# A written-out order for TensorE: one 512-column matmul of the running product behind each narrow matmul, and shorter planned landing times

## The chip, the cores and the metric

One core of a Trainium2 chip. The metric is the time of one launch on the device in microseconds (us); the median of three runs of the kernel before is 1319.29 us (1318.65 to 1319.43). A measurement of this kernel can tell about 0.2% from no change, which is 2.6 us.

## What is computed

One layer of a streaming encoder on 512 tokens of width 2048, in float32. Cut to what matters:

```python
hn   = rmsnorm(x, norm_g)                             # (512, 2048)
proj = hn @ w_in                                      # three branches of q, k, v, gate (4 heads of 128),
                                                      # forget logits, three merge gates of width 2048
ya = forgetting_attention(rmsnorm(qa), rmsnorm(ka), va, f_logit)   # branch A, causal, 4 heads
yb = chunked_relpos_attention(rmsnorm(qb), rmsnorm(kb), vb, rel)   # branch B, causal by chunks, 4 heads
yc = stick_breaking_attention(qc, kc, vc)                          # branch C, strictly causal, 4 heads
ys = stack(ya, yb, yc) * silu(gate paths)
merged = sum_n sigmoid(gates_n) * (ys_n @ w_up_n)
out = x + merged @ w_out
```

Twelve heads in all (three branches of four), each with a 512 x 512 causal score matrix.

## The kernel before, in words

**Wide matmuls.** Every large product is done in pieces: an operand is split into a high and a low part, and each block costs three matmuls (high by high, low by high, high by low). All of them go through one helper, `mm` (L264, L265), and have 128 rows, a stationary operand of 128 x 128 and 512 moving columns. I call them *wide*; there are 5328 of that helper. Weights arrive as `raw` tiles (512 KB each, eight buffers), ScalarE makes the high part `wh` (L366) and VectorE the low part `wl` (L371). The input projection is computed in 24 column groups of 512; from the third on, two groups at a time go through a seven-product scheme (`Strassen`, L580) whose products 5, 7 need the difference of two weight tiles: the first tile is fetched by SyncE's queue (`fetch`, L276), and the second is added onto it in memory by a GpSimd DMA with accumulation (`add_up`, L280). Sums of two weight tiles are made on VectorE (L574).

**Narrow matmuls.** Beside this running product each head needs TensorE for small steps: transposes of 128 x 128 blocks (`turned` L801 for q, k and the gate path, `soft_trans` L926 for the attention weights, `turned_m` L1282 for the merged result), score products with 128, 256, 384 or 512 columns for query blocks 0 to 3 (`mm3`, L260 to L262, and a mask product L898 in branch A), and the products of weights with values with 512, 384, 256 and 128 columns (`av`, L1014 to L1016). I call those of under 512 columns *narrow*: 328 transposes, 72 products each of 128, 256 and 384 columns, and 16 mask products.

**What sets the order.** The order of the instructions on TensorE, ScalarE and VectorE is fixed when the program is built. `Flow` (L65 to L148) is a small planner: every piece of work is a task, a Python generator that yields either something to wait for (an `Event`, buffer `Slots`) or a step `(engine, cost)`. `Flow.run` takes the step that can start first by its own clocks, and among equal starts the one due first (the time when it became ready plus the task's slack). The running product is one task with a slack of 1e9 (`stream`, L1412), so it takes what the others leave; the heads' tasks have a slack of 5.0, in the last head 0.3 to 4.0. The planner's costs are `mm_us` (L151), `act_us`, `dve_us`, and its guess of when a transfer lands is `landing` (L270) and `add_up` (L280). In the kernel before a step on TensorE is a whole small group: four transposes are one step of 0.44, the three matmuls of a score block are one step. On the chip every engine works through its list in order, and waits by semaphores.

**The stages.** About 5 to 970 us: the projection, with one head's attention under way beside the next group's product. About 970 to 1033: the last head's attention (branch A, head 3) and, when its products are through, the first of the products with `w_up`. About 1033 to 1160: four column groups of `w_up` with sigmoid gates; these gates were stored to memory earlier (`gl`), are fetched again as `sg`, go through a sigmoid on ScalarE (L1232) after a load of the table for it, and are multiplied with the product's PSUM tile on VectorE (L1248), which frees the tile (`taken`, L1244). There are four such tiles (`acc`), so the four token blocks of one branch's product wait for the four multiplies of the branch before, in the order in which VectorE makes them. Each column group ends with 16 transposes into four PSUM tiles `att` (`turned_m`). About 1160 to 1318: the product with `w_out` in two seven-product tasks.

Of the kernel before, what the change touches and what calls it, by code (L numbers as in the profile page):

```python
# [15 lines left out]
P = 128  # L16
# [48 lines left out]
class Flow:  # L65
# [84 lines left out]

def mm_us(n, x=1):  # L151
    return x * max(0.115, n / 2400 + 0.0133)

# [10 lines left out]
def hybrid_kernel(  # L164
# [92 lines left out]

    def mm3(ps, lh, ll, rh, rl, start, stop, more=False):

        nc.tensor.matmul(ps, lh, rh, start=start, stop=False, skip_group_check=more)  # L260
        nc.tensor.matmul(ps, lh, rl, start=False, stop=False, skip_group_check=more)  # L261
        nc.tensor.matmul(ps, ll, rh, start=False, stop=stop, skip_group_check=more)  # L262

# [111 lines left out]
    def products(u, ps, kts, tbs, block, first=False, last=False, bank=None, done=None, outer=False):  # L375

        for group in [[tb] for tb in tbs] if outer else [tbs]:
# [4 lines left out]
            for j, kt in enumerate(kts):  # L382
                for tb in group:
                    yield lambda: block(kt, tb) is not None
                    h, lo, ev = block(kt, tb)
                    yield ev
                    yield PE, mm_us(S, 2)
                    mm(ps[tb], h, u.hi[:, j, :], first and j == 0)
                    mm(ps[tb], lo, u.hi[:, j, :])
            yield u.ready  # L390
# [354 lines left out]
    class Head:  # L745
# [50 lines left out]
        def turned(self, r):  # L796

            yield PE, 0.11 * QB
            ps = att()
            for tb in range(QB):  # L800
                nc.tensor.transpose(ps[:, blk(tb)], self.c[tb][:, blk(r)], identf)  # L801
            self.taken()
            return ps
# [81 lines left out]
        def soft_scores(self, i):  # L885
# [5 lines left out]
            (qh, ql), (kh, kl) = self.t[Q], self.t[K]  # L891
            yield PE, mm_us(m, 3) + (mm_us(P) if n == A else 0)
            ps = att()[:, :m]
            mm3(ps, qh[:, blk(i)], ql[:, blk(i)], kh[:, :m], kl[:, :m], True, n == B)
            p = self.p[i]
            mx, sm = small("mx"), small("sm")
            if n == A:
                nc.tensor.matmul(ps[:, blk(i)], identb, mska, start=False, stop=True)  # L898
            done = self.nth("s", QB)
# [16 lines left out]
        def soft_trans(self, j):  # L916
# [5 lines left out]
            yield atts, 1  # L922
            yield PE, 0.11 * (QB - j)
            ps = att()
            for i in range(j, QB):
                nc.tensor.transpose(ps[:, blk(i)], self.p[i][:, blk(j)], identf)  # L926
            if self.nth("t", QB):
# [15 lines left out]
        def stick_scores(self, i):  # L943
# [4 lines left out]
            (qh, ql), (kh, kl) = self.t[Q], self.t[K]  # L948
            yield PE, mm_us(m, 3)
            ps = att()[:, :m]  # L950
            mm3(ps, qh[:, blk(i)], ql[:, blk(i)], kh[:, :m], kl[:, :m], True, True)
            if self.nth("s", QB):
# [49 lines left out]
        def av(self, j):  # L1002
# [4 lines left out]
            else:  # L1007
                yield atts, 1
            yield PE, mm_us(S - j * P, 3)
# [4 lines left out]
            nc.tensor.matmul(o, vh[:, blk(j)], h, start=j == 0, stop=False)  # L1014
            nc.tensor.matmul(o, vl[:, blk(j)], h, start=False, stop=False)  # L1015
            nc.tensor.matmul(o, vh[:, blk(j)], lo, start=False, stop=j == QB - 1)  # L1016
            set_(self.event("o", j))
# [59 lines left out]
    def quad(parts, g, done, early=False):  # L1077
# [8 lines left out]
        def mms(kts):  # L1086
            def go(u):
# [9 lines left out]
                else:  # L1097
# [3 lines left out]
                    for part in range(3):  # L1101
                        if part == 2:
                            yield u.ready
                        for j, kt in enumerate(kts):
                            yield (raw_hi[kt], raw_ev[kt], raw_ev[kt])[part]
                            yield PE, mm_us(S, QB)
                            w = u.lo if part == 2 else u.hi
                            for tb in tbs:
                                mm(ps[tb], block(kt, tb)[part == 1], w[:, j, :], kt + part == 0)
                if early and (kts[-1] + 1) % 4 == 0:  # L1110
# [92 lines left out]
    def split_y(i):  # L1203
        def go():
# [70 lines left out]
    def turned_m(g, i):  # L1275
        for tb in range(QB):
            yield merged_ev[NB - 1, g, tb]
        yield atts, 1
        yield PE, 0.11 * QB
        ps = att()  # L1280
        for tb in range(QB):
            nc.tensor.transpose(ps[:, blk(tb)], merged[g, tb][:, blk(i)], identf)  # L1282
        turns[g] = turns.get(g, 0) + 1
# [208 lines left out]
```

## Time and profile before

| | |
|---|---|
| median of the runs | 1319.29 us |
| the profiled execution | 1319.42 us, span 1317.7 us |
| TensorE busy | 1307.4 us (99%), 6034 matmuls |
| VectorE, ScalarE, GpSimd busy | 78%, 57%, 7% |
| TensorE idle by the trace | 6.1 us in five waits |
| granted TensorE clock | 1.000 |
| DMA | 266 MB, mean 202 GB/s |

How to read it. A row of the timeline has a start and a length in us, the engine, the line, the operation, what it writes and reads, the shapes and, after x, how many equal ones were merged. TensorE has two rows of records: PE for the matmuls and PEld for the load of the stationary operand that goes ahead of each. A matmul's recorded length (some 390 ns for a wide one) is longer than what it costs in a stream, since matmuls overlap; what one costs is read from start to start. A row ends with the engine's idle time ahead of it, in brackets, and what ended it.

### The profile page before, as it was taken

How to read it: one execution, taken by the hardware profiler on the slowest of the kernel's cores; microseconds unless marked ns; L12 is line 12 of the kernel's file. 1: busy time of each engine (PE TensorE's matmuls, PEld its weight loads, DVE VectorE, ACT ScalarE, POOL GpSimd, SP SyncE). 2: the span in 40 equal slices, each digit the busy share in tenths (PEclk: the TensorE clock that was granted, in tenths of full speed). 3: DMA queues.
4: the chain of work that ended last, by engine and by line, in shares of the span. 5: the costliest groups of instructions: out<-in, count | busy, mean ns of one | idle time of the engine just before them, and what ended most of it. 6: DMA issues, size and time to landing. Idle time of an engine off the chain costs nothing.

```text
span 1317.7 us, 17190 instructions
## 1 busy us (share of the span) xinstructions
PE 1307.4 (99%) x6034; PEld 1078.6 (82%) x6034; DVE 1023.4 (78%) x1420; ACT 752.4 (57%) x1271; POOL 91.5 (7%) x115
## 2 busy tenths in 40 slices
PE   9999999999999999999999999999999999999998
PEld 7788888888888888888888888888887788878787
DVE  6877787887878777687776877778789668798667
ACT  7655464564557646566466664667558545454342
POOL 0000001110011101111011110111000000000110
PEclk9999999999999999999999999999999999999999
DMA  9745677866777757777577775777786656637883
GB/s 361 233 121 145 181 210 191 235 170 180 211 192 229 201 164 232 175 228 203 170 225 176 225 207 168 224 177 217 225 250 196 236 192 205 164 95 250 246 240 128
DMA packets 89063, 266.03 MB, mean 202 GB/s; under 512 B 11264, under 2 KB 11264, under 8 KB 88976
## 3 DMA queue, kind: packets, MB, share of 16 engines
q1 hardware_dynamic: 71552, 206.16, 46.1%
q0 software_dynamic: 14976, 54.53, 23.2%
q10 hardware_dynamic: 2448, 4.24, 0.8%
q8 instruction: 47, 0.77, 0.2%
q14 instruction: 40, 0.33, 0.1%
HBM read 245.19 MB, written 19.70 MB: 201 GB/s over the span
## 4 chain that ended last, share of the span: by engine, by line
PE 95%; DMA 2%; ACT 1%; DVE 1%; issue 0%; POOL 0%; ACTq 0%; POOLq 0%; DVEq 0%
PE acc L265 87%; DMA raw<-in_w_out 2%; PE att L801 1%; PE att L926 1%; PE att L260 1%; PE att L261 1%; PE att L262 1%; DMA raw<-in_w_col 1%; PE att L1016 1%; PE att L1015 1%; PE att L1282 1%; ACT wh L366 1%; PE att L265 1%; PE att L1014 0%; DMA sg<-gl 0%; DVE wl L371 0%
## 5 line engine op out<-in xcount | busy, mean ns | idle before, releaser
L371 DVE TENSOR_TENSOR wl<-raw,wh 128x1024 fp32r<-128x1024 f32 (+1 forms) x405 | 493.4, 1220 | 209.5 <-PE acc L265 122.7
L366 ACT ACTIVATE wh<-raw 128x1024 fp32r<-128x1024 f32 (+1 forms) x405 | 426.7, 1055 | 369.5 <-PE acc L265 283.2
L265 PE MATMUL acc<-wh,x 128*128 128x512 f32 x1664 | 429.5, 392 | 0.0
L265 PEld LDWEIGHTS acc<-wh,x 128*128 128x128 f32 x1664 | 308.8, 188 | 65.7 <-ACT xn L476 1.7
L265 PE MATMUL acc<-wh,t 128*128 128x512 f32 x1056 | 272.7, 391 | 0.0
L265 PE MATMUL acc<-wl,x 128*128 128x512 f32 x832 | 230.1, 390 | 0.0
L265 PEld LDWEIGHTS acc<-wh,t 128*128 128x128 f32 x1056 | 196.7, 188 | 40.3
L265 PEld LDWEIGHTS acc<-wl,x 128*128 128x128 f32 x832 | 155.8, 188 | 33.0 <-DVE wl L371 0.4
L265 PE MATMUL acc<-wl,t 128*128 128x512 f32 x528 | 149.3, 390 | 0.0
L281 POOL DMA_DIRECT2D raw<-in_w_col x88 | 76.3, 867 | 878.1 <-DMA raw<-in_w_col 198.2
L574 DVE TENSOR_TENSOR raw<-raw,raw 128x1024 f32<-128x1024 f32 x104 | 126.7, 1218 | 0.0
L265 PEld LDWEIGHTS acc<-wl,t 128*128 128x128 f32 x528 | 98.4, 188 | 19.6
L265 PE MATMUL acc<-wh,m 128*128 128x512 f32 x416 | 105.2, 390 | 1.5 <-ACT wh L366 1.4
L265 PE MATMUL acc<-wh,y 128*128 128x512 f32 x384 | 103.7, 390 | 1.3 <-DVE sg L1248 1.3
L265 PEld LDWEIGHTS acc<-wh,m 128*128 128x128 f32 x416 | 77.9, 188 | 18.5 <-ACT wh L366 2.3
L265 PEld LDWEIGHTS acc<-wh,y 128*128 128x128 f32 x384 | 71.7, 188 | 16.8 <-DVE sg L1248 2.2
L265 PE MATMUL acc<-wl,y 128*128 128x512 f32 x192 | 59.7, 391 | 0.0
L265 PE MATMUL acc<-wl,m 128*128 128x512 f32 x208 | 58.1, 390 | 0.1
L246 ACT ACTIVATE ah<-att 128x512 fp32r<-128x512 f32 (+3 forms) x48 | 21.0, 438 | 48.1 <-PE att L926 48.1
L265 PEld LDWEIGHTS acc<-wl,m 128*128 128x128 f32 x208 | 38.9, 188 | 8.5 <-DVE wl L371 0.5
L250 DVE TENSOR_TENSOR al<-att,ah 128x512 fp32r<-128x512 f32 (+3 forms) x48 | 23.5, 490 | 25.5 <-ACT ah L246 24.8
L265 PEld LDWEIGHTS acc<-wl,y 128*128 128x128 f32 x192 | 35.7, 188 | 7.3
(179 smaller groups left out, 1115.9 us busy)
## 6 DMA issues: line engine op xcount, KB each, us to landing
raw<-in_w_col SPq DMA_DIRECT2D x235, 512.0 KB, 5.0
raw<-in_w_col POOLq DMA_DIRECT2D x88, 512.0 KB, 8.0
raw<-in_w_out SPq DMA_DIRECT2D x40, 512.0 KB, 3.6
raw<-in_w_up SPq DMA_DIRECT2D x24, 512.0 KB, 3.6
sg<-gl SPq DMA_DIRECT2D x48, 256.0 KB, 5.0
raw<-in_w_out POOLq DMA_DIRECT2D x16, 512.0 KB, 5.9
gl<-u SPq DMA_DIRECT2D x22, 256.0 KB, 9.2
gl<-s SPq DMA_DIRECT2D x22, 256.0 KB, 4.6
```

The costliest lines, as they stand in the source:

```text
L246: nc.scalar.activation(hi, src, AF.Copy)
L250: nc.vector.tensor_sub(lo, src, f(hi))
L260: nc.tensor.matmul(ps, lh, rh, start=start, stop=False, skip_group_check=more)
L261: nc.tensor.matmul(ps, lh, rl, start=False, stop=False, skip_group_check=more)
L262: nc.tensor.matmul(ps, ll, rh, start=False, stop=stop, skip_group_check=more)
L265: nc.tensor.matmul(ps, w, x, start=start, stop=stop, skip_group_check=more)
L281: nc.gpsimd.dma_start(to, src, accum_op=ALU.add)
L366: nc.scalar.activation(u.hi, u.raw, AF.Copy)
L371: nc.vector.tensor_sub(u.lo, u.raw, f(u.hi))
L574: nc.vector.tensor_add(to.raw, to.raw, self.raw)
L801: nc.tensor.transpose(ps[:, blk(tb)], self.c[tb][:, blk(r)], identf)
L926: nc.tensor.transpose(ps[:, blk(i)], self.p[i][:, blk(j)], identf)
```

## The change

The diff, cut to its core (the left-out pieces do the same to the other callers):

```diff
 class Flow:
+        self.main = None
+        self.narrow = False
...
     def spawn(self, gen, slack, ready=None):
+        if slack > 1e8:
+            self.main = task
...
     def run(self):
+            main = self.main
+            full = (self.narrow and main is not None and main.engine == PE
+                    and main.ready <= self.clock[PE] + 0.02)
             for t in self.tasks:
+                if full and t.engine == PE and t is not main and t.slack >= 1:
+                    continue
...
+            if e == PE:
+                self.narrow = t is not self.main and t.cost < 0.2

-def mm_us(n, x=1):
-    return x * max(0.115, n / 2400 + 0.0133)
+def mm_us(n):
+    return n / 2400 + 0.0133
+TURN = 0.05

-    def mm3(ps, lh, ll, rh, rl, start, stop, more=False):
+    def mm3(ps, lh, ll, rh, rl, start, stop, m):
         nc.tensor.matmul(ps, lh, rh, start=start, stop=False)
+        yield PE, mm_us(m)
         nc.tensor.matmul(ps, lh, rl, start=False, stop=False)
+        yield PE, mm_us(m)
         nc.tensor.matmul(ps, ll, rh, start=False, stop=stop)

     def add_up(to, src, ready, kb):
-        line[1] = max(line[1], ready + 1.0) + kb / 170.0
-        return Event(line[1] + 2.5)
+        line[1] += kb / 250.0
+        return Event(max(line[1], ready) + 6.5)

         def turned(self, r):
-            yield PE, 0.11 * QB
+            yield PE, TURN
             ps = att()
             for tb in range(QB):
+                if tb:
+                    yield PE, TURN
                 nc.tensor.transpose(ps[:, blk(tb)], self.c[tb][:, blk(r)], identf)

     def split_y(i):                 # in its branch for all heads but the last
+                yield heads[i].event("y")
                 yield t2s, 1
```

So each matmul becomes a step of its own in the planner (the wide ones and those of `av`, `soft_scores`, `soft_trans`, `turned_m` too). After a step outside the running product that is planned at under 0.2, a further step outside it is passed over as long as the running product has a matmul ready, unless the task's slack is under 1. A transpose is planned at 0.05 instead of 0.11, a 128-column product at 0.067 instead of 0.115. The planned landing of an accumulating DMA is still 6.5 after the first tile has landed when the line is free, but the planner's line of transfers is held for 2.05 instead of 3.01 per 512 KB, and no longer moved on to that landing plus one. What is computed, the number of instructions and the buffers are the same.

Counted over TensorE's whole list, the narrow matmuls stood in 122 groups between wide ones before and stand in 532 now: 313 single transposes, 66 single products each of 128, 256 and 384 columns, 12 single mask products, and 12 longer groups, mostly in the last head.

The first place is on TensorE at the last column group of `w_up`: `sg` are the merged tiles being transposed, `att` the PSUM tiles that they go to, and `acc` tiles belong to the running product with `w_out`. Before:

```order
L265 MATMUL acc_10273<-wl_10239,m_1812_9425 128x512
L1282 MATMUL att_10289<-identf,sg_9863 128x128
L1282 MATMUL att_10289<-identf,sg_9865 128x128
L1282 MATMUL att_10289<-identf,sg_9909 128x128
L1282 MATMUL att_10289<-identf,sg_9911 128x128
L1282 MATMUL att_10294<-identf,sg_9863 128x128
```

and now:

```order
L281 MATMUL acc_10273<-wl_10239,m_1818_9450 128x512
L1310 MATMUL att_10289<-identf,sg_9876 128x128
L281 MATMUL acc_10274<-wl_10239,m_1818_9450 128x512
L1310 MATMUL att_10292<-identf,sg_9876 128x128
L281 MATMUL acc_10273<-wl_10239,m_1821_9470 128x512
L1310 MATMUL att_10295<-identf,sg_9876 128x128
L281 MATMUL acc_10274<-wl_10239,m_1821_9470 128x512
L1310 MATMUL att_10300<-identf,sg_9876 128x128
L281 MATMUL acc_10273<-wh_10238,m_1823_9485 128x512
L1310 MATMUL att_10289<-identf,sg_9882 128x128
```

The 16 transposes stood in one piece and filled one PSUM tile after the other; now a wide matmul stands behind each, and the four tiles are filled side by side, so that the first is full with the thirteenth transpose instead of the fourth.

The second place is on TensorE in the last head: `p` are the attention weights, `y` marks wide matmuls of the product with `w_up`, `ah`, `al`, `vh`, `vl` are the parts of weights and values. Around its last transpose (L926, now L948) there stood:

```order
L265 MATMUL acc_9076<-wh_9024,y_8531 128x512 x2
L926 MATMUL att_9165<-identf,p_8837 128x128
L1014 MATMUL att_9116<-ah_9121,vh_8860 128x256
L1015 MATMUL att_9116<-ah_9121,vl_8861 128x256
L1016 MATMUL att_9116<-al_9122,vh_8860 128x256
L265 MATMUL acc_9076<-wh_9024,y_8569 128x512 x2
```

and now:

```order
L281 MATMUL acc_9089<-wl_9048,y_8572 128x512
L948 MATMUL att_9183<-identf,p_8842 128x128
L1037 MATMUL att_9134<-ah_9145,vh_8858 128x256
L1039 MATMUL att_9134<-ah_9145,vl_8859 128x256
L1041 MATMUL att_9134<-al_9146,vh_8858 128x256
L1037 MATMUL att_9134<-ah_9126,vh_8858 128x128
L1039 MATMUL att_9134<-ah_9126,vl_8859 128x128
L1041 MATMUL att_9134<-al_9127,vh_8858 128x128
L281 MATMUL acc_9204<-wh_9046,y_8599 128x512 x2
```

Counted from the start of the program, 4112 wide matmuls stand ahead of this transpose before and 4128 now; the narrow matmuls of the last head ahead of it are the same ones.

The third place is on ScalarE behind that transpose: `ah` is its copy out of PSUM, then come the table load and the sigmoids. Before:

```order
L246 ACTIVATE ah_9097<-att_9165 128x128
L1232 ACT_TABLE_LOAD
L1232 ACTIVATE sg_9123<-sg_9123 128x512
L1232 ACTIVATE sg_9125<-sg_9125 128x512
L1232 ACTIVATE sg_9127<-sg_9127 128x512
L1232 ACTIVATE sg_9129<-sg_9129 128x512
L246 ACTIVATE y_9136<-y_8961 128x2x256
L1232 ACTIVATE sg_9131<-sg_9131 128x512
L1232 ACTIVATE sg_9133<-sg_9133 128x512
L366 ACTIVATE wh_9206<-raw_8915 128x1024
L1232 ACTIVATE sg_9137<-sg_9137 128x512
L1232 ACTIVATE sg_9139<-sg_9139 128x512
```

and now:

```order
L260 ACTIVATE ah_9126<-att_9183 128x128
L1258 ACT_TABLE_LOAD
L1258 ACTIVATE sg_9147<-sg_9147 128x512
L1258 ACTIVATE sg_9149<-sg_9149 128x512
L1258 ACTIVATE sg_9151<-sg_9151 128x512
L1258 ACTIVATE sg_9153<-sg_9153 128x512
L260 ACTIVATE y_9103<-y_8947 128x2x256
L1258 ACTIVATE sg_9155<-sg_9155 128x512
L1258 ACTIVATE sg_9157<-sg_9157 128x512
L1258 ACTIVATE sg_9159<-sg_9159 128x512
L1258 ACTIVATE sg_9161<-sg_9161 128x512
L1258 ACTIVATE sg_9164<-sg_9164 128x512
```

The chain is the same but for one `wh`, which stood after the sixth sigmoid and now stands ahead of the `ah` of the first row. In both lists the ninth sigmoid (sg_9142, the row that follows those shown of before, and sg_9164, the last one shown now) is the one for VectorE's third multiply.

On SyncE's queue 19 of 501 rows have moved, most by one to four places; GpSimd's list is unchanged.

More of the change, by code (lines that the diff above doesn't have):

```diff
@@ L256, in minus @@
         nc.vector.scalar_tensor_tensor(to, a, -1.0, b, op0=ALU.mult, op1=ALU.subtract)
-    def mm3(ps, lh, ll, rh, rl, start, stop, more=False):
-        nc.tensor.matmul(ps, lh, rh, start=start, stop=False, skip_group_check=more)
-        nc.tensor.matmul(ps, lh, rl, start=False, stop=False, skip_group_check=more)
-        nc.tensor.matmul(ps, ll, rh, start=False, stop=stop, skip_group_check=more)
+    def mm3(ps, lh, ll, rh, rl, start, stop, m):
+        nc.tensor.matmul(ps, lh, rh, start=start, stop=False)
+        yield PE, mm_us(m)
+        nc.tensor.matmul(ps, lh, rl, start=False, stop=False)
+        yield PE, mm_us(m)
+        nc.tensor.matmul(ps, ll, rh, start=False, stop=stop)
     def mm(ps, w, x, start=False, stop=False, more=False):
@@ L386, in products @@
                     yield ev
-                    yield PE, mm_us(S, 2)
+                    yield PE, mm_us(S)
                     mm(ps[tb], h, u.hi[:, j, :], first and j == 0)
+                    yield PE, mm_us(S)
                     mm(ps[tb], lo, u.hi[:, j, :])
@@ L891, in soft_scores @@
             (qh, ql), (kh, kl) = self.t[Q], self.t[K]
-            yield PE, mm_us(m, 3) + (mm_us(P) if n == A else 0)
+            yield PE, mm_us(m)
             ps = att()[:, :m]
-            mm3(ps, qh[:, blk(i)], ql[:, blk(i)], kh[:, :m], kl[:, :m], True, n == B)
+            yield from mm3(ps, qh[:, blk(i)], ql[:, blk(i)], kh[:, :m], kl[:, :m], True, n == B, m)
             p = self.p[i]
@@ L922, in soft_trans @@
             yield atts, 1
-            yield PE, 0.11 * (QB - j)
+            yield PE, TURN
             ps = att()
             for i in range(j, QB):
+                if i > j:
+                    yield PE, TURN
                 nc.tensor.transpose(ps[:, blk(i)], self.p[i][:, blk(j)], identf)
@@ L948, in stick_scores @@
             (qh, ql), (kh, kl) = self.t[Q], self.t[K]
-            yield PE, mm_us(m, 3)
+            yield PE, mm_us(m)
             ps = att()[:, :m]
-            mm3(ps, qh[:, blk(i)], ql[:, blk(i)], kh[:, :m], kl[:, :m], True, True)
+            yield from mm3(ps, qh[:, blk(i)], ql[:, blk(i)], kh[:, :m], kl[:, :m], True, True, m)
             if self.nth("s", QB):
@@ L1008, in av @@
                 yield atts, 1
-            yield PE, mm_us(S - j * P, 3)
+            n = mm_us(S - j * P)
+            yield PE, n
             if j == 0:
@@ L1278, in turned_m @@
         yield atts, 1
-        yield PE, 0.11 * QB
+        yield PE, TURN
         ps = att()
         for tb in range(QB):
+            if tb:
+                yield PE, TURN
             nc.tensor.transpose(ps[:, blk(tb)], merged[g, tb][:, blk(i)], identf)
```

5 lines of the change are left out of this document (4 added, 1 removed).

## The prediction, made blind

> **What bounds the kernel now.** I read the page first, then the waits of TensorE, then the timeline around narrow matmuls, and last the places where TensorE waits.
>
> ```profile
> span 1317.7 us, 17190 instructions
> PE 1307.4 (99%) x6034; PEld 1078.6 (82%) x6034; DVE 1023.4 (78%) x1420; ACT 752.4 (57%) x1271; POOL 91.5 (7%) x115
> ...
> PE att L417 <- DVE identb L310: 1.9, 1, 1.9
> PE acc L265 <- ACT wh L366: 1.4, 1, 1.4
> PE acc L265 <- DVE sg L1248: 1.3, 1, 1.3
> PE att L265 <- DVE wl L371: 1.1, 1, 1.1
> PE att L801 <- ACT w L793: 0.4, 1, 0.4
> ```
>
> TensorE is the bound all the way: it waits five times, 6.1 us together, and 1.9 of them are the start. So the change can pay in two ways only: a narrow matmul gets cheaper on TensorE, or one of the four later waits goes. It can cost in the same two ways. The price of a wide and of a narrow matmul is read from start to start (the first row is from the chain that ended last, the others from the timeline):
>
> ```profile
> 118.90 43.59 PE acc L265 x192
> ...
> 115.25 0.27 PE L926 MATMUL att<-identf,p 128*128 128x128 f32 x1
> 115.28 0.36 PE L1014 MATMUL att<-ah,vh 128*128 128x256 f32 x1
> 115.48 0.28 PE L1015 MATMUL att<-ah,vl 128*128 128x256 f32 x1
> 115.60 0.28 PE L1016 MATMUL att<-al,vh 128*128 128x256 f32 x1
> ...
> 115.03 0.14 PEld L926 LDWEIGHTS att<-identf,p 128*128 128x128 f32 x1
> 115.26 0.19 PEld L1014 LDWEIGHTS att<-ah,vh 128*128 128x128 f32 x1
> 115.36 0.19 PEld L1015 LDWEIGHTS att<-ah,vl 128*128 128x128 f32 x1
> ...
> 1053.54 1.08 PE L265 MATMUL acc<-wh,y 128*128 128x512 f32 x4
> 1054.46 1.91 PE L1282 MATMUL att<-identf,sg 128*128 128x128 f32 x16
> 1056.12 0.70 PE L265 MATMUL acc<-wl,y 128*128 128x512 f32 x2
> 1056.66 0.63 PE L265 MATMUL acc<-wh,y 128*128 128x512 f32 x2
> ...
> 63.03 0.40 PE L265 MATMUL acc<-wh,x 128*128 128x512 f32 x1
> 63.26 0.60 PE L801 MATMUL att<-identf,c 128*128 128x128 f32 x4
> 63.62 0.71 PE L265 MATMUL acc<-wh,x 128*128 128x512 f32 x2
> 64.17 0.86 PE L265 MATMUL acc<-wl,x 128*128 128x512 f32 x3
> ```
>
> A wide one costs 43.59 / 192 = 0.227. From 1053.54 to 1056.66 lie six wide ones (1.36) and 16 transposes, so those cost 1.76, or 0.110 each. That is twice what their 128 columns would cost by the wide rate (a 256-column product takes 115.60 - 115.48 = 0.12, a wide one 0.107 more for 256 more columns, so 128 columns should take about 0.066).
>
> The middle rows are the case that the change makes everywhere: a single transpose with a wide matmul ahead of it and a broader one behind. Its weights were loaded from 115.03 on, in the shadow of the wide one ahead of it. But the load for the matmul behind it starts at 115.26, a hundredth after the transpose itself, though the load unit had been free for a while, and the next load starts 0.10 later. From the transpose to the second 256-column product it takes 115.48 - 115.25 = 0.23, and 0.12 of that is the first such product. So the single transpose still costs 0.11: the load behind it has only the transpose to hide under, and it is longer than that. A narrow matmul pays for the load that comes after it, not for its own, whatever stands there.
>
> **TensorE's own work.** The change leaves the numbers of matmuls as they are: 328 transposes and 72 products of 128 columns at 0.11. What it changes is the number of groups, 122 to 532. A change between narrow and wide costs a little: the 16 transposes took 1.76, which is 0.01 over 16 x 0.109; the four at 63.26 took 64.17 - 63.03 - 3 x 0.227 = 0.46, which is 0.02 over 4 x 0.109. Of the 410 new groups 287 have a 128-column matmul in them, at 0.01 each 2.9. The other 123 are single products of 256 and 384 columns, long enough to cover a load; I take half the price, 0.6. Sum +3.5. Bounds: nothing, if the price belongs to a long stretch and not to each group; 410 x 0.023 = 9.4 by the group of four. I take the price of the sixteen, since its two ends are measured over the longer stretch, and by the single transpose above (0.11 in all) the price cannot be much higher.
>
> **The wait for the sigmoids.** It ends with the second row here:
>
> ```profile
> 1024.06 0.27 PE L926 MATMUL att<-identf,p 128*128 128x128 f32 x1
> ...
> 1033.01 1.19 PE L265 MATMUL acc<-wh,y 128*128 128x512 f32 x4 [1.28 <-DVE sg L1248]
> ...
> 1024.37 0.28 ACT L246 ACTIVATE ah<-att 128x128 fp32r<-128x128 f32 x1 [1.65 <-PE att L926]
> 1024.66 1.28 ACT L1232 ACT_TABLE_LOAD   x1
> ...
> 1029.62 1.05 ACT L366 ACTIVATE wh<-raw 128x1024 fp32r<-128x1024 f32 x1
> 1030.57 3.22 ACT L1232 ACTIVATE sg<-sg 128x512 f32<-128x512 f32 x6
> ...
> 1032.26 1.29 DVE L1248 TENSOR_TENSOR sg<-acc,sg 128x512 f32<-128x512 f32 x2 [1.12 <-ACT sg L1232]
> ```
>
> The chain is: the last head's last transpose (1024.06), its copy on ScalarE, the table load, nine sigmoids with a `y` and a `wh` among them, the third multiply on VectorE (1032.26), the PSUM tile, TensorE at 1033.01. In the new order that transpose has 16 more wide matmuls ahead of it (4128 for 4112), 16 x 0.227 = 3.6 later, because the four blocks' score products now take turns and end together, and the softmax and the transposes behind them start later. On ScalarE the chain behind it is shorter by the `wh` (1030.57 - 1029.62 = 0.95). The wait ends 3.6 - 0.95 = 2.7 later, and the wide matmuls that TensorE has until then are the same ones, merely done earlier, so nothing covers it: +2.7. Queued behind the late sigmoids on ScalarE are the `wh` of the units two ahead, with some 5 us to spare. Bounds: -1.5, if the whole wait went (no reason for it in the order), and +3.6 without the `wh`.
>
> **Two other waits.** The first row below starts four transposes that wait for ScalarE's scaling; they and the wide one behind them cost 998.54 - 997.05 (996.14 + 4 x 0.227), which is 1.05 over 4 x 0.11. Now wide matmuls stand between them and the first waits one wide matmul longer, but the others not at all: -0.3.
>
> ```profile
> 996.14 1.08 PE L265 MATMUL acc<-wh,x 128*128 128x512 f32 x4
> 997.58 0.62 PE L801 MATMUL att<-identf,w 128*128 128x128 f32 x2 [0.36 <-ACT w L793]
> ...
> 998.54 0.71 PE L265 MATMUL acc<-wl,x 128*128 128x512 f32 x2
> ...
> 1171.83 1.07 PE L265 MATMUL att<-wh,m 128*128 128x512 f32 x4
> 1174.03 1.19 PE L265 MATMUL att<-wl,m 128*128 128x512 f32 x4 [1.13 <-DVE wl L371]
> ...
> 1172.16 0.69 DVE L250 TENSOR_TENSOR m<-m,m 128x512 fp32r<-128x512 f32 x1
> 1172.76 1.22 DVE L371 TENSOR_TENSOR wl<-raw,wh 128x1024 fp32r<-128x1024 f32 x1
> ```
>
> The wait at 1174.03 costs 1174.03 - 1171.83 - 4 x 0.227 = 1.3. It is VectorE's queue: five splits of merged tiles (`m`, 0.6 each from 1172.16 to 1172.76) stand ahead of that `wl`. Now the four PSUM tiles fill side by side, so these tiles come later, and the new list has none of the five ahead of that `wl`. 5 x 0.6 = 3.0 less in the queue covers 1.3, but the first copy out of PSUM comes some 12 x 0.34 - 3 x 0.11 = 3.7 later and leaves VectorE fewer things to do meanwhile. I take the wait as gone, -1.3, with +1 as the other bound.
>
> **The planned landing times** move little but the planner's opinion: SyncE's list keeps its order but for 19 rows, GpSimd's is the same, and the loads wait for free `raw` tiles on the chip. The wait for the second `w_out` task is a chain of two transfers of about 10 us each (rows of the chain); its start is a `wl` that follows TensorE's own progress, so it stays: 0, give or take 1.5.
>
> ```profile
> 1223.12 9.65 DMA raw<-in_w_out
> ...
> 1233.33 10.52 DMA raw<-in_w_out
> ...
> raw<-in_w_col POOLq DMA_DIRECT2D x88, 512.0 KB, 8.0
> ```
>
> **The sum.** 3.5 + 2.7 - 0.3 - 1.3 = +4.6 on the profiled execution's 1319.42 (a span of 1317.7 and 1.7 around it), 1324.0; the median of the runs, 1319.29, is 0.13 below, so 1323.9. About 0.2%, or 2.6 us, is what a measurement here can tell.
>
> **The rivals.**
>
> *The narrow matmuls get cheap.* If TensorE can hold the load for the matmul after next while a wide one runs, a narrow matmul between wide ones costs only its columns, 0.066 instead of 0.11. Then 400 x 0.044 = 17.6 goes, and with +1.1 from the waits the time is 1302.8. Against it: the load rows at 115.26 and 115.36, and in all the trace no load that runs two ahead. For it: a single transpose with a wide (not a 256-column) matmul behind it is not in the trace. The Trainium skill, "TensorE: Matmul & The Clock Gate", section "Back-to-back issue gap", speaks for this rival: it gives about 56 ns for a matmul of 128 columns by itself and about 81 ns in a stream of loads and matmuls, pipelined through a reorder window. By these figures the time would come out as an estimated 1299 to 1309; the trace's 0.11 for a single transpose agrees with neither. My chance for this rival is 0.08.
>
> *No change that can be told.* The price of a change belongs to stretches (0 instead of 3.5): 1319.3 + 1.1 = 1320.4. Or both terms are half of what I reckon: 1319.3 + 1.75 + 1.35 - 1.6 = 1320.8. For it: the price was read from hundredths of a microsecond; against it: both groups show it with the same sign. 0.22.
>
> *Much slower.* The planner now thinks TensorE faster (0.05 for 0.11) and an accumulating DMA to land 6.5 after the first tile, where the last row above says 8.0 from issue to landing; ScalarE and VectorE work in order, so a `wh` put too early holds all behind it. TensorE is two units (5 us) behind these, so single delays of 1.5 are covered; were one of 1 us in each of the eleven later heads not, it is 1323.9 + 11 = 1335; were the price of a change the 0.023 of the group of four, 1319.3 + 9.4 + 1.1 = 1329.8. Against it: ScalarE waits for these transfers now too, without TensorE waiting for ScalarE there. 0.10.
>
> That the change does not do what it says is excluded by the order: 313 single transposes stand between wide matmuls.
>
> **How the numbers follow.** Forecast 0.60, cheap 0.08, no change 0.22, much slower 0.10. Faster by over 0.2% are the first rival and 0.03 of the forecast, should several waits go that I leave standing: 0.11; within 0.2% are the 0.22; slower is the rest, 0.67. The range 1317.5 to 1330.5 leaves out the cheap case, the last of the good luck and half of the much slower one.
>
> **What would show it.** In the new profile: the start of a wide matmul behind a single transpose comes about 0.12 later than without the transpose, so a pair of both takes about 0.35 (0.29 if the first rival is right); the load behind it starts with the transpose; TensorE's wait for `sg` has grown from 1.3 to about 4, in one or two places; the wait for `wl` at the start of `w_out` is gone; the wait for `raw` near the second task is still there. If pairs take 0.29, the whole prediction is wrong; if they take 0.35 and the time is below 1321, the sigmoid chain is where to look.

## The result, and the profile after

The changed kernel takes 1324.46 us (median of 5 runs, 1324.09 to 1327.19), the kernel before beside it 1319.29. The ratio is 1.0042, with a 95% interval of 1.0029 to 1.0056. The forecast was 1323.9. The profiled execution took 1324.79 (span 1323.1).

The head of the page, and then the waits of TensorE (in all, how often, the longest):

```profile
span 1323.1 us, 17158 instructions
PE 1310.8 (99%) x6034; PEld 1073.6 (81%) x6034; DVE 1023.0 (77%) x1420; ACT 754.2 (57%) x1271; POOL 91.5 (7%) x115
...
PE acc L281 <- DVE sg L1274: 3.3, 2, 1.7
PE att L434 <- DVE identb L326: 1.9, 1, 1.9
PE acc L281 <- ACT wh L382: 1.1, 1, 1.1
PE acc L281 <- DVE wl L387: 0.8, 1, 0.8
PE att L1037 <- ACT ah L260: 0.4, 1, 0.4
PE att L281 <- DVE wl L387: 0.3, 1, 0.3
PE att L1041 <- DVE al L264: 0.2, 1, 0.2
PE att L281 <- ACT wh L382: 0.2, 1, 0.2
```

The two pages differ by 32 instructions (17190 before): all of them are semaphore instructions, and every engine's own work has the same number of instructions. TensorE is busy 3.4 us longer for the same 6034 matmuls, and waits 8.2 us instead of 6.1. The wait for the sigmoids grew from 1.3 to 3.3. The 1.1 for `wl` at the start of `w_out` and the 0.4 for `w` went. Five small rows stand for waits at new places.

What a wait costs, and what the matmuls cost among themselves, can be read together from one series: the start of the k-th wide matmul of the helper `mm`, of which all kernels have the same 5328. The table gives that start for the kernel before, and for other kernels how much later it comes (us; the other kernels are those of the experiments below):

| k | before | after | rule off | landing alone | old prices | longer turns | turns whole | gates first | rule in heads |
|---|---|---|---|---|---|---|---|---|---|
| 0 | 6.14 | +0.21 | +0.20 | -0.43 | +0.20 | +0.21 | +0.21 | -0.01 | +0.21 |
| 20 | 10.80 | +0.70 | +0.68 | -0.42 | +0.62 | +0.59 | +0.79 | -0.04 | +0.67 |
| 4000 | 991.12 | +3.16 | +0.97 | -0.06 | +3.11 | +3.05 | +3.25 | +0.28 | +3.13 |
| 4040 | 1002.74 | +1.60 | -0.62 | -1.65 | +1.52 | +2.42 | +1.86 | -1.31 | +1.55 |
| 4152 | 1035.86 | +4.96 | +1.60 | -0.98 | +4.63 | +4.46 | +5.37 | -2.52 | +2.67 |
| 4660 | 1156.37 | +5.32 | +1.58 | -0.98 | +5.00 | +4.83 | +5.34 | -2.52 | +2.64 |
| 4700 | 1167.21 | +5.47 | +1.61 | -0.98 | +5.15 | +4.98 | +5.37 | -2.52 | +2.67 |
| 4730 | 1175.53 | +3.95 | +1.28 | -0.99 | +3.63 | +3.46 | +4.71 | -2.54 | +2.02 |
| 4850 | 1202.73 | +6.08 | +1.30 | -0.98 | +7.28 | +5.22 | +4.71 | -2.54 | +2.02 |
| 5327 | 1313.33 | +5.40 | +1.40 | -1.88 | +6.04 | +4.21 | +4.09 | -3.14 | +0.97 |

Read down the column "after": 0.70 is lost by k = 20, ahead of any narrow matmul of a head. The loss then grows while the heads' narrow matmuls alternate with wide ones (to k = 4000), changes in steps in the last head (4000 to 4152), grows a little with the 64 transposes of the merged product (to 4700), falls where the `wl` wait was, and rises again soon after.

Two cautions on the table. First, a row compares like with like only where as many narrow matmuls lie ahead of it. That is so in every row but k = 4040: there the kernel before has done four transposes more than all the others, which is 0.44 of each fall from 4000 to 4040. Second, the loss by k = 20 is one of the clock. The trace's record of the granted clock begins, at full, 5.91 us after the start in the kernel before and 7.44 in the changed one, and the first wide matmuls of the latter start 0.57, 0.43 and 0.28 apart, then 0.23. In all six traces of kernels built on the changed one that record begins at 7.15 to 7.64, in the four others at 4.80 to 6.23. No run here shows what sets it.

The alternation itself, at the last transposes of the merged product. First TensorE's matmuls, then its loads of stationary operands:

```profile
1162.84 0.27 PE L1310 MATMUL att<-identf,sg 128*128 128x128 f32 x1
1162.87 0.48 PE L281 MATMUL acc<-wl,m 128*128 128x512 f32 x1
1163.19 0.27 PE L1310 MATMUL att<-identf,sg 128*128 128x128 f32 x1
```

```profile
1162.84 0.19 PEld L281 LDWEIGHTS acc<-wl,m 128*128 128x128 f32 x1
1162.97 0.14 PEld L1310 LDWEIGHTS att<-identf,sg 128*128 128x128 f32 x1
1163.19 0.19 PEld L281 LDWEIGHTS acc<-wl,m 128*128 128x128 f32 x1
```

A pair takes 1163.19 - 1162.84 = 0.35 (0.344 over longer stretches), not 0.29, and the load of the wide one's operand starts with the transpose. A lone transpose costs 0.344 - 0.227 = 0.117.

The sigmoid wait, on TensorE, ScalarE and VectorE:

```profile
1029.62 0.27 PE L948 MATMUL att<-identf,p 128*128 128x128 f32 x1
...
1033.29 1.19 PE L281 MATMUL acc<-wh,y 128*128 128x512 f32 x4 [1.66 <-DVE sg L1274]
...
1037.97 1.20 PE L281 MATMUL acc<-wh,y 128*128 128x512 f32 x4 [1.65 <-DVE sg L1274]
```

```profile
1029.35 1.06 ACT L382 ACTIVATE wh<-raw 128x1024 fp32r<-128x1024 f32 x1 [0.43 <-PE acc L281]
1030.31 0.26 ACT L260 ACTIVATE ah<-att 128x128 fp32r<-128x128 f32 x1
1030.59 1.28 ACT L1258 ACT_TABLE_LOAD   x1
1031.88 2.19 ACT L1258 ACTIVATE sg<-sg 128x512 f32<-128x512 f32 x4
```

```profile
1037.23 1.29 DVE L1274 TENSOR_TENSOR sg<-acc,sg 128x512 f32<-128x512 f32 x2 [1.91 <-ACT sg L1258]
```

The last transpose comes 5.56 later than before; without the 3.16 that TensorE was late already, 2.4. The `wh` that no longer stands among the sigmoids stands ahead of the `ah` now and keeps it until 1030.31, 0.69 after the transpose, where it was 0.31 before. The third multiply comes 4.97 later.

### The profile page after: what moved, and what is told of

Read it like the earlier page. It is cut to its first block, busy times and chain, and to the rows that moved or that the text cites. A ratio compares the mean times of both kernels' runs of the same rounds, so it can differ in the third digit from the quotient of the medians.

```text
span 1323.1 us, 17158 instructions
## 1 busy us (share of the span) xinstructions
PE 1310.8 (99%) x6034; PEld 1073.6 (81%) x6034; DVE 1023.0 (77%) x1420; ACT 754.2 (57%) x1271; POOL 91.5 (7%) x115
## 4 chain that ended last, share of the span: by engine, by line
PE 98%; DVE 1%; ACT 1%; issue 0%; POOL 0%; DVEq 0%; ACTq 0%; POOLq 0%
PE acc L281 91%; PE att L820 1%; PE att L948 1%; PE att L281 1%; DVE wl L387 1%; PE att L276 1%; PE att L278 1%; PE att L1310 1%; PE att L274 1%; PE att L1037 1%; PE att L1041 1%; PE att L1039 1%; ACT sg L1258 0%; PE att L434 0%; PE att L1141 0%; ACT wh L382 0%
## 5 line engine op out<-in xcount | busy, mean ns | idle before, releaser
L281 PE MATMUL acc<-wh,x 128*128 128x512 f32 x1664 | 456.8, 402 | 0.0
L281 PE MATMUL acc<-wh,t 128*128 128x512 f32 x1056 | 283.5, 393 | 0.0
L281 PE MATMUL acc<-wl,x 128*128 128x512 f32 x832 | 233.6, 393 | 0.0
L281 PE MATMUL acc<-wh,y 128*128 128x512 f32 x384 | 106.9, 397 | 3.3 <-DVE sg L1274 3.3
```

The lines of the kernel that those rows point to most:

```text
L281: nc.tensor.matmul(ps, w, x, start=start, stop=stop, skip_group_check=more)
```

## The experiments

There were two theories at the start: **load** (the alternation itself costs TensorE time, and it delays the last head's transposes, so the rule is the cause) against **planner** (the new prices or landing times put ScalarE's and VectorE's work in a worse order).

**1. The rule off** (the changed kernel, its steps and prices kept; the narrow matmuls stand in 157 groups):

```diff
-            full = (self.narrow and main is not None and main.engine == PE
+            full = (False and main is not None and main.engine == PE
```

> The changed kernel without the rule that puts a wide matmul behind each narrow one; its single steps, planned costs and planned landing times stay. By the order the narrow matmuls then stand in 157 groups instead of 532 (135 instead of 400 with a 128-column matmul in them), and the last head's last transpose has 4121 wide matmuls ahead of it instead of 4128. Load theory (a narrow matmul pays for the weight load behind it, and each group costs about 0.01 us at its ends): 265 x 0.01 + 110 x 0.005 = 3.2 us less on TensorE, and the sigmoid wait ends up to 7 x 0.227 = 1.6 us earlier: 1324.5 - 3.2 - 1.6 = 1319.7, between 1318.5 and 1321.3. Planner theory (the alternation itself costs nothing; the new planned costs and landing times put ScalarE's and VectorE's work in a worse order): nothing that it names is undone, so 1323.5 or more.

Measured: 1319.83 (1318.66 to 1320.80), ratio 1.0000 (0.9991 to 1.0009). All of the loss is gone, with the prices and landing times still in. Load stands. In the table this column still ends at +1.40: its trace, the slowest of these runs, has 0.68 of that by k = 20, and from 1031.42 us its granted clock stands at half for 3.41 us (the mean from 1030 to 1040 is 0.83, in the kernel before and the changed one 1.00).

**2. The landing times alone** (the kernel before with the new `add_up`):

```diff
-        line[1] = max(line[1], ready + 1.0) + kb / 170.0
-        return Event(line[1] + 2.5)
+        line[1] += kb / 250.0
+        return Event(max(line[1], ready) + 6.5)
```

> The kernel before with the changed kernel's planned landing of accumulating DMAs alone. By the order there are 136 groups instead of 122, and the last head's last transpose has 4114 wide matmuls ahead instead of 4112. Load theory: 14 x 0.01 + 2 x 0.227 = 0.6 us more, 1319.9, between 1319 and 1321. Planner theory with the landing times as the cause: the larger part of the 5.2 us, 1322 or more.

Measured: 1318.03 (1317.51 to 1319.18), ratio 0.9988 (0.9979 to 0.9997). A small gain, where 1319.9 (1319 to 1321) was expected. The table shows its places. Between k = 4000 and 4040 it falls by 1.6; 0.44 of this is the four transposes still to come, the rest is the wait of the last head's transposes for ScalarE's scaling, and over the whole last head (to 4152) 0.9 remains. Another 0.9 goes at the second `w_out` task. There two traces of one kernel, that of experiment 6, differ by 0.4, so the size of this second part is not certain.

**3. The old prices** (the changed kernel with 0.11 for a transpose and 0.115 as the least for a product; still 532 groups):

```diff
-    return n / 2400 + 0.0133
+    return max(0.115, n / 2400 + 0.0133)
-TURN = 0.05
+TURN = 0.11
```

> The changed kernel with the old planned prices of narrow matmuls (0.115 at least, 0.11 for a transpose), the rule and the landing times as changed. The order of narrow and wide matmuls is the same in number: 532 groups, 4128 wide ones ahead of the last head's last transpose; ScalarE's and VectorE's lists differ. Load theory: TensorE's own work and the sigmoid wait stay, 1324.5 give or take 1.2 for the waits in the last product. Planner theory with the prices as the cause: with prices that fit the chip the order is good again, 1321.5 or less.

Measured: 1325.01 (1323.35 to 1325.45), ratio 1.0037 (1.0024 to 1.0050). That is within the 1324.5 give or take 1.2 of the load theory. The prices are not the cause; planner falls.

**4. Longer turns in the last head** (there a task of the last head with a slack under 1 keeps its due time for a further step on TensorE, so that the blocks' products no longer take turns; the last transpose has 4118 wide ones ahead of it):

```diff
                 task.engine, task.cost = w[:2]
+                if task.slack < 1 and task.engine == task.prev == PE:
+                    return
```

> The changed kernel, but in the last head (slack under 1) a step on TensorE that follows another one of the same task keeps that one's due time, so the four blocks' score products no longer take turns. By the order 529 groups, and the last transpose has 4118 wide matmuls ahead instead of 4128. Load theory with the sigmoid chain: the same price on TensorE, and the wait for the sigmoids ends up to 10 x 0.227 = 2.3 us earlier: 1322.2, between 1321.7 and 1323.3, with TensorE's wait for the gate tiles at 1 to 2 us instead of 3.3. If that wait is not set by this transpose: 1324.5.

Measured: 1323.07 (1321.43 to 1324.56), ratio 1.0026 (1.0017 to 1.0034); the wait for `sg` is 2.5 us. The time lies in the range expected, but near its end, and the wait is longer than the 1 to 2 expected. The rows on ScalarE say why:

```profile
1028.96 1.28 ACT L1260 ACT_TABLE_LOAD   x1
1030.25 0.63 ACT L1260 ACTIVATE sg<-sg 128x512 f32<-128x512 f32 x1
1030.95 0.63 ACT L262 ACTIVATE y<-y 128x512 fp32r<-128x512 f32 x1
1031.49 1.05 ACT L384 ACTIVATE wh<-raw 128x1024 fp32r<-128x1024 f32 x1
1032.44 5.81 ACT L1260 ACTIVATE sg<-sg 128x512 f32<-128x512 f32 x11
```

The table load starts 1.63 earlier than in the changed kernel, but a `y` and a `wh` (1.5 together) now stand ahead of nearly all sigmoids. And the wait for ScalarE's scaling came partly back (+2.42 at k = 4040 in the table, for +1.60).

**5. The turns of the merged product whole.** The rise between k = 4730 and 4850 was in no term of the forecast. The changed kernel shows there, on TensorE, VectorE, ScalarE and on SyncE's loading queue:

```profile
1206.41 0.73 PE L281 MATMUL acc<-wl,m 128*128 128x512 f32 x2 [0.81 <-DVE wl L387]
```

```profile
1186.14 1.22 DVE L591 TENSOR_TENSOR raw<-raw,raw 128x1024 f32<-128x1024 f32 x1
...
1188.21 1.22 DVE L591 TENSOR_TENSOR raw<-raw,raw 128x1024 f32<-128x1024 f32 x1
...
1203.39 0.69 DVE L672 TENSOR_TENSOR u<-u,xr 128x512 f32<-128x512 f32 x1 [1.51 <-DMA xr<-in_xn]
1204.01 2.35 DVE L387 TENSOR_TENSOR wl<-raw,wh 128x1024 fp32r<-128x1024 f32 x2
```

```profile
1203.24 1.06 ACT L382 ACTIVATE wh<-raw 128x1024 fp32r<-128x1024 f32 x1 [2.77 <-DMA raw<-in_w_out]
```

```profile
1166.56 27.02 SPq L293 DMA_DIRECT2D raw<-in_w_out  x5
```

So `wl` waits for `wh` and for `xr`, both wait for transfers, and the queue that issues them stood most of 27 us for five blocks. Its own waits between 1160 and 1215 say for what, in the changed kernel and in the kernel before:

```profile
SPq L293 <- DVE raw L591: 35.1, 4, 15.6
...
SPq L277 <- DVE raw L574: 41.4, 5, 15.9
```

These are VectorE's sums of `raw` tiles, the two at 1186.14 and 1188.21 above. The queue stands as long for them in the kernel before; what differs is when they come. There the same two are:

```profile
1179.47 1.22 DVE L574 TENSOR_TENSOR raw<-raw,raw 128x1024 f32<-128x1024 f32 x1
...
1181.91 1.22 DVE L574 TENSOR_TENSOR raw<-raw,raw 128x1024 f32<-128x1024 f32 x1
```

They come 6.7 and 6.3 later, TensorE only 3.95. The order of the queue differs too. In the kernel before the first `xr` stands ahead of the fifth block, in the changed kernel behind it (first before, then now), and so it is issued 9.7 later:

```profile
1163.68 19.86 SPq L277 DMA_DIRECT2D raw<-in_w_out  x4
1183.94 0.33 SPq L277 DMA_DIRECT2D xr<-in_xn  x1
...
1193.67 0.98 SPq L293 DMA_DIRECT2D xr<-in_xn  x2
```

The edit puts the four transposes of a tile in one piece again, too long for the rule:

```diff
-        yield PE, TURN
+        yield PE, TURN * QB
         ps = att()
         for tb in range(QB):
-            if tb:
-                yield PE, TURN
             nc.tensor.transpose(ps[:, blk(tb)], merged[g, tb][:, blk(i)], identf)
```

> The changed kernel, but the transposes of the merged product (64 in all) stand four in a piece again, planned at 0.2 us for a piece, so that the rule leaves them alone. What it is to tell: where the two waits of 2.1 us in all come from that the changed kernel's TensorE has 31 to 45 us after the last of these transposes, and that no term of the forecast held. Theory (spread transposes): one to a 512-column matmul, the last 16 take 15 more such matmuls (3.4 us) to be done; the splits of the product follow late, the sums of raw blocks stand behind them on VectorE, the loading queue waits for those, and blocks of w_out land late. Then with the pieces whole the two waits go (-2.1), the wait for wl of the kernel before comes back in front of them (+1.4), and 48 groups fewer give 0.4 back: 1324.5 - 1.1 = 1323.4 (1322.9 to 1323.9). Rival (the shorter planned landing times place these loads too late): the waits stay and only the 0.4 is seen, 1324.1.

Measured: 1322.60 (1321.36 to 1323.74), ratio 1.0022 (1.0013 to 1.0031). Three rows of TensorE's waits in it:

```profile
PE att L434 <- DVE identb L326: 1.9, 1, 1.9
PE acc L281 <- ACT wh L382: 1.2, 1, 1.2
PE att L281 <- DVE wl L387: 0.6, 1, 0.6
```

and the same two sums:

```profile
1184.90 1.22 DVE L591 TENSOR_TENSOR raw<-raw,raw 128x1024 f32<-128x1024 f32 x1
...
1187.51 1.22 DVE L591 TENSOR_TENSOR raw<-raw,raw 128x1024 f32<-128x1024 f32 x1
```

The sums are 5.4 and 5.6 later than before, TensorE 4.71. The rise is gone: between k = 4730 and 4850 the table has +4.71 and +4.71. The `wl` wait came back at half its size. The median is below the range expected (1322.9 to 1323.9): it differs by 1.9 from the changed kernel's, not by 1.1; by the table the end is 1.3 earlier. Spreading the transposes is the cause of the rise. By which way is open: the edit brings the sums forward, and it also puts the loading queue back in the order of the kernel before. The rise stands in the three traces with the moved order (changed kernel, experiments 3 and 4) and in none of the others. That late sums and late loads lead to it is read from the traces; the two were not tried apart.

This trace, too, has a stretch of half clock: 3.41 us from 1035.05, just behind the first sigmoid wait. Four wide matmuls take 1036.80 - 1035.09 = 1.71 there, 0.43 each:

```profile
1035.09 1.91 PE L281 MATMUL acc<-wh,y 128*128 128x512 f32 x4
1036.80 1.05 PE L281 MATMUL acc<-wl,y 128*128 128x512 f32 x2
```

It hides most of the second sigmoid wait, which is 0.41 in this trace instead of 1.65.

**6. Block C's gates first** (kernel before, new landing times, and in `gates_of` the first column group's other gates take a tile only when C's four have one):

```diff
+        if g == 0 and n != C:
+            for e in first_gates:
+                yield e
         yield t2s, 1
         t = sig[n, g, tb] = t2("sg")
+        if g == 0 and n == C:
+            set_(first_gates[tb])
```

> The kernel before with the new landing times, and one thing of its own: of the first column group's twelve gates, the four that are multiplied first (block C) take their tiles, and so their places in ScalarE's list, ahead of the other eight; before, two of the four stood ninth and tenth. Theory (TensorE waits there for the sigmoids' order, not for their start): the sigmoid wait of 1.7 us goes and nothing takes its place, 1318.0 - 1.7 = 1316.3 (1315.8 to 1317.0), 0.9975 of the kernel before. Rival (ScalarE has too much there in any order, so the next block's gates are late instead): 1317.5 to 1318.2, with a wait for sg a few us further on.

Measured: 1316.60 (1315.74 to 1317.15), ratio 0.9977 (0.9967 to 0.9986). The row for the sigmoids among TensorE's waits:

```profile
PE acc L265 <- DVE sg L1254: 0.2, 1, 0.2
```

It was their order, not how many there are. This version is faster than both kernels, by 3.0 than the kernel before.

**7. What is left: the rule in the heads**, that is the changed kernel with the edits of 5 and 6; and beside it kernel 6 again. The two differ by the rule and by the rest of the change but the landing times: the single steps, the planned prices and the new wait in `split_y`.

> The changed kernel with the transposes of the merged product in pieces of four (as one run before) and with block C's four gates first (as in another): what is left of the change is the alternation of the heads' narrow matmuls. Theory (the sum's terms are separate): the second of the two sigmoid waits goes here too (-1.7), the first stays, since the last transpose is still late: 1322.6 - 1.7 = 1320.9 (1320.3 to 1321.5), and 4.3 more than the kernel before with the new landing times and the gates first (1316.6), of which 3.2 are TensorE's own work in the alternation and the rest waits in the last head and after it. Rival (with the sigmoids 6 us late, their order doesn't matter): 1322.6, sigmoid waits still 2 us.

> The kernel before with the new landing times and block C's gates first, once more, on the same chip as the run beside it, so that the two differ by the alternation alone: 1316.6 (1316.0 to 1317.2) if the first figure holds; 1317.5 or more if that was luck.

Measured: 1322.02 (1319.91 to 1323.02), ratio 1.0017 (1.0008 to 1.0026); kernel 6 again 1316.62 (1315.12 to 1317.96), 0.9977 (0.9968 to 0.9985). The row for the sigmoids in the first:

```profile
PE acc L281 <- DVE sg L1280: 1.7, 1, 1.7
```

One of the two waits is left, as the theory has it, but the median lies between theory and rival, outside the 1320.3 to 1321.5 expected: it is 0.6 under that of experiment 5, where the profiled executions differ by 3.1 (1320.37 for this one, 1323.49 for that one). The granted clock is a large part of this. Of the 11 runs here the three with a mean of 1.000 took 1319.91 to 1320.51, the eight with 0.997 to 0.999 took 1321.38 to 1323.02. The profiled one is of the first kind and has no stretch of half clock in the last head; that of experiment 5 has one. Among the runs of experiment 5 the two kinds do not part so (1322.30 and 1322.45 at 1.000), so the rest is open. Kernel 6 held. The rule with its steps and prices costs 4.0 by the profiled executions (1320.37 against 1316.33), 0.5 of it by k = 20 in the clock's start (+0.67, and +0.13 in this second trace of kernel 6), and 5.4 by the medians.

**8. Pairs by themselves.** A kernel that computes nothing of the layer, only matmuls in stretches, run once; the granted clock is 1.00 in all the stretches below.

> Nothing of the layer is computed: matmuls alone, in stretches. 80 of 512 columns; 40 pairs of a transpose and one of 512 columns; 10 times four transposes and four of 512; 40 of 512 columns with only 32 stationary columns; 40 pairs of a transpose and one of these; 40 pairs of a 128-column product and one of 512; the same with 32 stationary columns; 40 pairs of a 256-column product and one of 512; 40 of 512. What it is to tell: what a lone narrow matmul between two wide ones costs. Theory (it lasts as long as the load of the next stationary operand, which begins when it begins): pair of transpose and 512 columns 0.34 us (0.227 + 0.117), the same for the 128-column product; four and four 1.36 (4 x 0.227 + 0.447); a pair with only 32 stationary columns behind falls to about 0.29, if a load of a quarter of the columns takes about a quarter of the time; 256 columns and 512 0.35. Rival (the 0.117 is the narrow matmul's own time or a price of changing the width): 0.34 for the pair with 32 stationary columns too.

The first row of each stretch (L42 wide, L45 the same with 32 stationary columns, L48 a transpose, L51 a product):

```profile
24.45 0.27 PE L48 MATMUL ps<-identf,a 128*128 128x128 f32 x1
...
38.15 0.38 PE L48 MATMUL ps<-identf,a 128*128 128x128 f32 x2
...
51.85 0.62 PE L45 MATMUL pq<-bh,ah 128*32 128x512 f32 x2
...
61.04 0.27 PE L48 MATMUL ps<-identf,a 128*128 128x128 f32 x1
...
74.84 0.22 PE L51 MATMUL ps<-bh,ah 128*128 128x128 f32 x1
...
88.45 0.22 PE L51 MATMUL ps<-bh,ah 128*128 128x128 f32 x1
...
99.93 0.28 PE L51 MATMUL ps<-bh,ah 128*128 128x256 f32 x1
```

Each stretch lasts until the next row: 40 pairs of transpose and wide 13.70, or 0.3425 each; ten times four and four 13.70, or 1.370 each; 40 with 32 stationary columns 9.19, 0.230 each; 40 pairs of a transpose and one of these 13.80, 0.345; of a 128-column product and a wide one 13.61, 0.340; of a product and one with 32 stationary columns 11.48, 0.287. The last stretch shown, pairs of a 256-column product and a wide one, lasts 14.12, 0.353 each. So a lone 128-column product costs 0.340 - 0.227 = 0.113 with a whole load behind it and 0.287 - 0.230 = 0.057 with a short one: it does pay for the load behind it, as the theory has it. A lone transpose costs 0.115 either way: for it, the theory falls and the rival stands.

## Why the prediction was right, point by point

**TensorE's own work, +3.5: measured 3.0.** From k = 20 to 4000 the loss grows by 2.46 (0.70 to 3.16), and the 64 transposes of the merged product add 0.51 (4.96 to 5.47; whole, in experiment 5, they add nothing). The price of a group was right in size. Taken from the wide matmul ahead to the second one behind, less 0.2266 for each wide one, as medians over all such places: four transposes cost 0.447 in a piece and 0.471 one by one, 0.024 for three groups more; 16 cost 1.758 and 1.873, 0.115 for 15 more. The split by size was off: single 256-column products cost 0.128 where three in a piece cost 0.120 each, and 384-column ones nothing more.

**Its explanation was half right.** The rows quoted at 115.26 fit a narrow matmul that pays for the load behind it, and for products experiment 8 shows it. For transposes, which are most of the groups, the load is not the limit. What the limit is, no run here shows.

**The start, 0: measured +0.7.** The sum had no term for it. It is the later start of the full clock, and whether it comes with the changed kernel or by chance no run here shows.

**The wait for the sigmoids, +2.7, and the scaling wait, -0.3: together +2.4 forecast, +1.8 measured** (3.16 to 4.96). They are not two terms: the scaling wait lies ahead of the last transpose, so what TensorE saves there brings the transpose forward. The scaling wait went whole: the loss falls by 1.56 between k = 4000 and 4040, of which 0.44 is the four transposes still to come and 1.1 the wait. The step that failed is "the first waits one wide matmul longer": no one of the four waits now. And this is no merit of the alternation: the landing times alone remove the same wait (experiment 2). That the wait would grow "to about 4, in one or two places" came as two of 1.66 and 1.65.

**The wait for `wl`, -1.3: measured -1.5** (4700 to 4730 in the table, +5.47 to +3.95). The cause given fits, since with the transposes in pieces 0.6 of it came back.

**What was missed, +2.1** (3.95 to 6.08). I followed the late `m` tiles to the one `wl` that they no longer hold up, and stopped there. VectorE's sums of `raw` tiles also come late in this kernel, and so do the loads, whose order has moved as well. The step that failed is "with +1 as the other bound": the bound was looked for at the same wait, not at what else stands in that queue. And "SyncE's list keeps its order but for 19 rows" passed over rows that matter: the first `xr` behind the fifth block is among them.

**The landing times, 0: measured -1.5 by themselves** (1318.03 beside 1319.54). "Move little but the planner's opinion" was wrong: the new order is worth more than a microsecond, at two waits. In the changed kernel the wait near the second task costs 0.7 less (+6.08 to +5.40), within the 1.5 given and not much more than the 0.4 by which two traces of one kernel differ there.

So 0.7 + 3.0 + 1.8 - 1.5 + 2.1 - 0.7 = +5.4, the last row of the table, in the place of +4.6. The two main terms, TensorE's own work and the sigmoid wait, were right in kind and near in size. That the sum came so close is partly luck: losses of 2.8 that it did not hold (the start 0.7, the loads 2.1) met four terms that came out 2.0 lower together (TensorE's work 0.5, the last head 0.6, the `wl` wait 0.2, the second task 0.7).

**The rivals.** Cheap narrow matmuls: excluded, the pair takes 0.344. The Trainium skill, "TensorE: Matmul & The Clock Gate", section "Back-to-back issue gap", gives about 56 ns for a 128-column matmul by itself and about 81 in a stream. Experiment 8 has 0.057 for a product, but only with 32 stationary columns behind it, and 0.081 in no stretch. No change: excluded by the interval (1.0029 at least). Much slower: TensorE has no wait above 0.1 us in the heads' stretch up to k = 4000, and the price of a change is 0.008 for transposes, not 0.023.

## What to carry to other kernels

An order that alternates short and long matmuls helps only if the short ones then wait less or cost less. Measure a pair first (0.344 for 0.227 + 0.110 here), because hundreds of groups at 0.008 each add up (3.0 us here), and here to more than any one wait that the kernel had. Where a group feeds other engines, spreading it delays its last member by all that is put between (16 transposes 3.4 us), and everything behind that must be followed: the queues of the engines that take it, the buffers that they free, and the loads that wait for these and their order. A wait for one item in a queue of a dozen is often a matter of their order: four gates moved ahead of eight gave 1.4 us here.

## What the runs showed that was not expected

The wide matmuls just behind a group are slower too: in the stretch of four and four they start 0.230 to 0.237 apart by the single starts, instead of 0.227. So 40 transposes in pieces of four cost there as much as 40 alone (1.370 per four pairs, and 4 x 0.3425). In the layer long runs of wide ones follow each group, and the piece of four is cheaper.

The granted clock of this one core is not always full: it stands at half for 3.41 us in the last head in the traces of experiments 1 and 5. Up to half of that, 1.7 us, can stand between two profiled executions for this alone, and the rows from start to start show it (0.43 for 0.227).

The Trainium skill, "TensorE: Matmul & The Clock Gate", section "LDWEIGHTS (loading the stationary operand)", says that a load's time goes by the number of stationary columns; the fall from 0.113 to 0.057 for the product, with 32 columns in place of 128 behind it, agrees.
